# A transformer block with product-key experts: bf16 gate tables, a shorter candidate list, and another spread of gathered rows

## The chip, the cores and the metric

The kernel runs on one core of a Trainium2 chip. The metric is the device time of one launch in microseconds. TensorE multiplies matrices and writes PSUM, VectorE and ScalarE do elementwise work, GpSimd issues the indirect gathers and some other transfers, and SyncE issues most loads. Each engine works through its own instructions in order and waits on semaphores for the others.

## The reference

One layer on 528 frames (16 meta tokens ahead of 512 frames) of width 2048: two attention branches with gates, an output projection, and then the part that this change touches, a product-key expert layer (PEER), followed by a last RMSNorm. For each of the 512 tokens and each of 8 heads:

```
q  = (xb @ w_q)                        # 8 heads, two halves of 128
s  = q . sub_keys                      # per head two lists of 128 scores
s1, i1 = top_k(s[0], 16); s2, i2 = top_k(s[1], 16)
cand   = s1[:, None] + s2[None, :]     # 256 sums
top_s, pos = top_k(cand, 16)
idx = (i1[:, None] * 128 + i2[None, :])[pos]      # 16 of 16384 experts
g   = softmax(top_s)
h   = u[idx] . xb ;  act = g * gelu(h)
out = sum(act * v[idx])
```

So every token uses 8 x 16 = 128 experts of 16384, each with a row of `u` and a row of `v` of 2048 fp32 values (128 MB for each of the two tables). Both sorted lists fall, so the 16 highest sums (a, b) have (a + 1)(b + 1) <= 16.

## The kernel before

The kernel goes through the stages one after another: projections and stick-breaking attention, MLA attention, the branch products, the output projection, the routing scores, and two long expert phases. Every fp32 product is made of three fp32r matmuls on high and low halves (`mm3`, L230 to L232): ScalarE rounds a raw weight tile to the high half `wh` (L218), VectorE subtracts it for the low half `wl` (L219), and both are ready some tiles ahead of TensorE (four raw buffers, three of `wh` and `wl` and one more from an extra pool).

The expert layer is done in two ways. For `ND` = 342 of the 512 tokens (tiles 0, 1 and 2, the last one 86 tokens long) it is dense: all of `u` and all of `v` pass through TensorE, and the chosen experts come in as a gate matrix of 16384 experts by 342 tokens that is zero but for 128 entries a token. The other 170 tokens (128 of tile 3 and 42 spread over 126 partitions) gather their rows: `send` (L1135) fetches row k of each token by an indirect transfer on GpSimd's queue, and `row_step` multiplies it on VectorE, for `u` with a sum (L1148) and for `v` added into `xg` or `xgb` (L1152). There are 171 row steps for `u` and 171 for `v`.

The first phase (the loop over `e`, 128 turns) takes the tiles of `u`: two half tiles a turn, each 24 matmuls with 342 columns, a GELU on ScalarE and a store to `h_d`. Beside it run generators, of which the loop takes a step at fixed places:

- `routing` (`route`, for tiles 2, 0 and 1, two heads at a time). It forms the 256 sums `cand` (L889), takes the 16 highest in two rounds of eight with `top16` (five scans, L853 to L857), splits each place by shift and mask into its two indices, and finds the keys by one-hot comparison, product and sum (L901, L903, L905). Tile 3 is routed earlier, beside the scores, as `early`.
- `gating` (`gates_of`). For four tokens VectorE compares the two key lists with an iota (L1043, `[2, 4, 128]` in fp32), ScalarE scales the first one-hot by the high and low part of the weight (L1040), and TensorE multiplies, per token, the one-hot of the second keys as the stationary operand with the two scaled ones (L1051), which gives 128 x 128 gates in a bank of PSUM, with the tokens outermost. `gate_out` copies a bank to SBUF with the tokens innermost (L1073) and sends it to `g_d`.
- `rows_due`, which calls `row_step` so that the number of row steps follows the piecewise line `PACE` over the position in the loop: 10 by position 14, 175.5 by 124, `NU` = 181 at the end, so ten steps of `v` fall into this phase. Up to row `OWN` = 172 the buffers of the second phase serve as row buffers; behind it there are two.

The second phase (`STEPS`, 256 blocks of two columns) takes the tiles of `v`, multiplies them with the gated activations (`gated`, L1180 and L1182; `group_split`, L236) and adds into `acc` (L1321, L1323). Its row steps follow `(done - NU) * 484 / (342 - NU)` over the count n of columns, with a third row buffer from the pool `vp` for every third row. After step 490 TensorE folds `yvb` and `yv` in, and the final norm follows.

The order of instructions on each engine is made by a list scheduler from the order of recording and from the buffers; order that the text forces with `add_manual_dep` (rows behind a mark, gate work behind the GELU) is kept.

Of the kernel before, what the change touches and what calls it, by code (L numbers as in the profile page):

```python
# [57 lines left out]

CONST = {}


def _constants():
    p = np.arange(P)
    cols = {
        "ident": np.eye(P),
        "ones": np.ones((P, P)),
        "tri": (p[:, None] >= p[None, :]),
        "perm": (p[:, None] == (p[None, :] ^ 32)),
        "neg": np.where(p[None, :] <= p[:, None], NEG, 0.0),
        "qlo": np.where(p[None, :] < 64, 1.0, 0.0) * np.ones((P, 1)),  # L70
        "negrow": np.full((P, 64), NEG),
        "freq": (10000.0 ** (-((p % 32) / 32.0)))[:, None],
        "sign": np.where(p % 64 < 32, -1.0, 1.0)[:, None],
        "iota": np.arange(TOPK)[None, :] * np.ones((P, 1)),
        "sel": (p[:, None] // RB == np.arange(NB)[None, :]),
        "eps": np.full((P, 1), EPS),
        "halfpi": np.full((P, 1), math.pi / 2),
    }
    out, o = [], 0
    for k, v in cols.items():  # L80
        v = np.asarray(v, np.float64).astype(np.float32)
        CONST[k] = (o, o + v.shape[1])
        o += v.shape[1]
        out.append(v)
    return np.ascontiguousarray(np.concatenate(out, axis=1))

# [29 lines left out]
def _layout(x, positions, meta_tokens, norm_mix_g, w_in, mla_q_norm_g, mla_w_uq, mla_kv_norm_g,  # L116
# [50 lines left out]
    for i, n in enumerate(FRONT):  # L167
# [9 lines left out]
    return {"front": front, "ut": c(ut), "vb": c(vb), "u": c(u), "v": c(v), "xt": c(xt),  # L177
            "pos": c(pos[None]), "gains": c(gains), "const": CONST_ARR,
            "iota": c(np.broadcast_to(np.arange(P, dtype=np.float32), (P, P)))}
# [12 lines left out]
def body(tc, nc, a, dbg=None):  # L192
# [56 lines left out]
    SP.dma_start(gn, a["gains"])  # L249
    cst = cp.tile([P, CONST_ARR.shape[1]], F32, name="cst")  # L250

    def C(k):
        return cst[:, CONST[k][0]:CONST[k][1]]

# [29 lines left out]
    mixer = ExitStack()  # L284
    mp = mixer.enter_context(tc.tile_pool(name="mixer", bufs=1, side="left"))
    tri_r = mp.tile([P, P], F32R, name="tri_r")
    ones_r = mp.tile([P, P], F32R, name="ones_r")
# [31 lines left out]
    with tc.tile_pool(name="load", bufs=3, side="right") as lp:  # L319
# [31 lines left out]
    SP.dma_start(cst, a["const"])  # L351
    V.tensor_copy(tri_r, C("tri"))
# [434 lines left out]
    hgl = hgp.tile([P, KC, SEQ], F32R, name="hgl")  # L787
    rh_ = hgp.tile([P, SEQ], F32, name="rh_")
    rcol = hgp.tile([P, 1], F32, name="rcol")
    rcolb = hgp.tile([P, 1], F32, name="rcolb")  # L790

    with tc.tile_pool(name="outp", bufs=2, side="right") as op:
# [8 lines left out]
        for m in range(KC):  # L801
# [23 lines left out]
            gr = (op if m < KC - 1 else hgp).tile([P, 2, P], F32, name="gr")  # L825
            V.tensor_scalar(gr[:, 0], xr[:, TA:], gm, None, ALU.mult)
# [39 lines left out]
    def spread_rows():  # L866
# [10 lines left out]
        SP.dma_start(gwb[:PB], gwb_d.rearrange("t (r k) -> (t r) k", r=RB))  # L877

    def route(ti, n, pool):
        shp = [P, n, TOPK, TOPK]  # L880
        tv = pool.tile([P, H, TOPK], F32, name="tv", bufs=1)
        ef = keys[ti] = pool.tile([P, 2, H, TOPK], F32, name="ef", bufs=1)
        for h0 in range(0, H, n):
            hs = slice(2 * h0, 2 * (h0 + n))
            vv, ii = (t[:, ti, hs].rearrange("p (h c) k -> p h c k", c=2) for t in (v1, i1))
            i1f = pool.tile([P, n, 2, TOPK], F32, name="i1f", bufs=1)
            V.tensor_copy(i1f, ii)
            cand = pool.tile([P, n, TOPK, TOPK], F32, name="cand", bufs=1)
            V.tensor_tensor(cand, vv[:, :, 0, :, None].to_broadcast(shp), vv[:, :, 1, None, :].to_broadcast(shp), ALU.add)  # L889
            yield  # L890
            tp = pool.tile([P, n, TOPK], U32, name="tp", bufs=1)
# [3 lines left out]
            for c, (op_, arg) in enumerate(((ALU.logical_shift_right, 4), (ALU.bitwise_and, 15))):  # L895
                pu = pool.tile([P, n, TOPK], U32, name="pu", bufs=1)
                pf = pool.tile([P, n, TOPK], F32, name="pf", bufs=1)
                V.tensor_scalar(pu, tp, arg, None, op_)
                V.tensor_copy(pf, pu)
                oh = pool.tile([P, n, TOPK, TOPK], F32, name="oh", tag="cand", bufs=1)  # L900
                V.tensor_tensor(oh, pf[:, :, :, None].to_broadcast(shp), iota[:, None, None, :].to_broadcast(shp), ALU.is_equal)  # L901
                yield
                V.tensor_tensor(oh, oh, i1f[:, :, c, None, :].to_broadcast(shp), ALU.mult)  # L903
                yield
                V.reduce_sum(ef[:, c, h0:h0 + n], oh, axis=AX.X)  # L905
                yield
        e_ = pool.tile([P, H, TOPK], F32, name="e_", bufs=1)
# [15 lines left out]
    with tc.tile_pool(name="score", bufs=2, side="left") as sp_, \  # L923
# [9 lines left out]
        def scores(hc, qh, ql):  # L933
# [10 lines left out]
            if hc % 4 == 3:  # L944
                for _ in range(9):
                    next(early, None)
# [63 lines left out]

    iota_n = up.tile([P, P], F32, name="iota_n", bufs=1)
    SP.dma_start(iota_n, a["iota"])
    iota_b = iota_n[:, None, None, :].to_broadcast([P, 2, 4, P])
    gb = {}

    spare = [t[:, :, ND:ND + P].rearrange("p (i c t) k -> p i c t k", i=2, c=2) for t in (hgh, hgl)]

# [4 lines left out]
    def gates_of(ti):  # L1022
        ef, idx = keys[ti], up.tile([P, 2, P], F32, name="idx", bufs=1)
        wt = up.tile([P, 2, P], F32R, name="wt", bufs=1)
# [4 lines left out]
        S.activation(idx, ps[:, :2 * P].rearrange("p (c t) -> p c t", c=2), AF.Copy)  # L1029
        split(wt[:, 0], wt[:, 1], ps[:, 2 * P:3 * P])  # L1030
        yield
        n = min(P, ND - ti * P)
        for t0 in range(0, n + 4, 4):
            w, w_ = min(4, n - t0), min(4, n - t0 + 4)
            if t0:
                p0 = t0 - 4
                oh_, wo_ = (spare[c][:, p0 // 4 % 2] for c in range(2))
                for t in range(w_):
                    for c in range(2):
                        after_gelu(S.activation(wo_[:, c, t], oh_[:, 0, t].bitcast(F32), AF.Copy,  # L1040
                                                scale=wt[:, c, p0 + t:p0 + t + 1].bitcast(F32)))
            if w > 0:
                V.tensor_tensor(spare[0][:, t0 // 4 % 2, :, :w], idx[:, :, t0:t0 + w, None].to_broadcast([P, 2, w, P]),  # L1043
                                iota_b[:, :, :w], ALU.is_equal)
            yield
            gate_out()
            if t0:
                ps = ps_tile()
                for t in range(w_):
                    for c in range(2):  # L1050
                        T.matmul(ps[:, t * P:(t + 1) * P], oh_[:, 1, t], wo_[:, c, t], start=c == 0, stop=c == 1)  # L1051
                banks.append((ps, ti * P + p0, w_))
            yield
            if w_ < 4:
                break

# [3 lines left out]
    def gate_out(hold=3):  # L1060

        for _ in range(min(2, len(banks))):
# [9 lines left out]
            for hf, half in enumerate(gb["now"]):  # L1072
                after_gelu(S.activation(half[:, :, o:o + w].rearrange("p i t -> p t i"),  # L1073
                                        ps.rearrange("p (t f i) -> p f t i", t=4, f=2)[:, hf, :w], AF.Copy))
# [194 lines left out]
    for i, step in enumerate(STEPS):  # L1269
# [17 lines left out]
        for qi, (g, q8) in enumerate(step):  # L1287
# [18 lines left out]
            for dc in range(2):  # L1306
# [46 lines left out]
```

## Time and profile before

| | |
|---|---|
| median of three runs | 3632.78 us (3629.29 to 3633.52) |
| profiled execution | 3635.84 us, span 3634.1 us |
| mean granted TensorE clock | 0.994 |
| matmuls | 21139, busy 3573.3 us |
| VectorE, ScalarE, GpSimd busy | 2609.7, 1466.1, 743.5 us |
| moved | 890 MB, 245 GB/s over the span |
| first expert phase | about 1541 to 2626 us |
| second expert phase | about 2626 to 3600 us |

The profile is one execution. Its page groups instructions by source line, engine and operation and gives for each group the count, the busy time, the mean of one in ns, and the time in which the engine stood idle just before them with what ended that. A busy time by stretch gives the same for windows of the span, with the clock that TensorE was granted and the share of the DMA engines' time. Matmuls overlap in the pipeline, so the time that one occupies TensorE is read from the distance of two starts in the timeline and not from its length.

### The profile page before, as it was taken

The numbers are of one execution on the slowest core, as the hardware profiler recorded it, in microseconds if no ns is written. First come the engines' busy times: TensorE is split into PE (matmuls) and PEld (weight loads), VectorE is DVE, ScalarE is ACT, GpSimd is POOL, SyncE is SP. The second block draws the span as 40 slices with busy tenths as digits, with TensorE's granted clock in tenths as the row PEclk, the third lists the DMA queues.
The fourth block names the chain that finished last, engine by engine and source line by source line (L and its number), as shares of the span: only waits on it lengthen the run. The fifth ranks groups of instructions, "written<-read, shape, count | busy, mean of one in ns | idle before, by whom it ended". The sixth has DMA issues, their size and how long they took to land.

```text
span 3634.1 us, 53241 instructions
## 1 busy us (share of the span) xinstructions
PE 3573.3 (98%) x21139; PEld 3323.5 (91%) x21139; DVE 2609.7 (72%) x3431; ACT 1466.1 (40%) x2336; POOL 743.5 (20%) x523
## 2 busy tenths in 40 slices
PE   9999999999999999999999999999999999999998
PEld 8988888888788887899999999999999999999997
DVE  5533334345554558799999988887688988888886
ACT  4233323334443233234665666664323333333333
POOL 1000000000011122211232323333123333332320
PEclk9999999999999999999999999999999999999999
DMA  4222222221134443268899999999999999999983
GB/s 169 102 96 99 93 99 93 94 101 47 46 131 136 148 146 104 93 251 327 320 361 346 353 375 370 362 378 381 346 372 379 380 379 376 373 370 374 373 339 113
DMA packets 218385, 889.97 MB, mean 245 GB/s; under 512 B 24644, under 2 KB 47384, under 8 KB 174360
## 3 DMA queue, kind: packets, MB, share of 16 engines
q1 hardware_dynamic: 133016, 462.87, 35.0%
q0 software_dynamic: 56608, 384.51, 27.0%
q10 hardware_dynamic: 28512, 39.20, 3.0%
q8 instruction: 165, 2.70, 0.3%
q14 instruction: 84, 0.69, 0.1%
HBM read 824.18 MB, written 62.30 MB: 244 GB/s over the span
## 4 chain that ended last, share of the span: by engine, by line
PE 83%; DVE 9%; DMA 5%; issue 2%; ACT 1%; POOL 0%; SPq 0%; DVEq 0%; ACTq 0%; POOLq 0%
PE ps L230 26%; PE ps L231 26%; PE ps L232 26%; DVE row L1148 2%; DMA row<-v,eo 2%; DVE wl L219 2%; PE ps L1051 1%; DVE xg L1152 1%; DVE hgh L1043 1%; DMA hin<-h_d 1%; DMA wr<-vb 1%; DMA wr<-ut 0%; PE ps L707 0%; PE ps L716 0%; DMA hres<-ht_d 0%
## 5 line engine op out<-in xcount | busy, mean ns | idle before, releaser
L218 ACT ACTIVATE wh<-wr 128x1024 fp32r<-128x1024 f32 (+1 forms) x756 | 789.6, 1054 | 1505.9 <-PE ps L232 1313.5
L219 DVE TENSOR_TENSOR wl<-wr,wh 128x1024 fp32r<-128x1024 f32 (+1 forms) x741 | 935.7, 1268 | 440.7 <-ACT wh L218 438.6
L230 PE MATMUL ps<-hgh,wl 128*128 128x342 f32 (+1 forms) x2304 | 759.0, 329 | 17.8 <-DVE wl L219 15.4
L231 PE MATMUL ps<-hgl,wh 128*128 128x342 f32 (+1 forms) x2304 | 761.0, 330 | 0.9 <-DVE hgl L236 0.9
L232 PE MATMUL ps<-hgh,wh 128*128 128x342 f32 (+1 forms) x2304 | 755.0, 328 | 0.0
L230 PE MATMUL ps<-vah,wl 128*128 128x342 f32 x2048 | 657.9, 321 | 12.2 <-DVE wl L219 12.2
L231 PE MATMUL ps<-val,wh 128*128 128x342 f32 x2048 | 655.7, 320 | 0.0
L232 PE MATMUL ps<-vah,wh 128*128 128x342 f32 x2048 | 654.2, 320 | 0.0
L230 PE MATMUL ps<-xh,wl 128*128 128x512 f32 (+1 forms) x1376 | 470.3, 342 | 6.1 <-ACT xh L323 6.1
L231 PE MATMUL ps<-xl,wh 128*128 128x512 f32 (+1 forms) x1376 | 470.0, 342 | 0.2 <-DVE xl L324 0.2
L232 PE MATMUL ps<-xh,wh 128*128 128x512 f32 (+1 forms) x1376 | 468.0, 340 | 0.0
L230 PEld LDWEIGHTS ps<-hgh,wl 128*128 128x128 f32 x2304 | 435.3, 189 | 34.7 <-DVE wl L219 20.7
L232 PEld LDWEIGHTS ps<-hgh,wh 128*128 128x128 f32 x2304 | 436.2, 189 | 11.0 <-issue 0.2
L231 PEld LDWEIGHTS ps<-hgl,wh 128*128 128x128 f32 x2304 | 436.0, 189 | 11.1 <-DVE hgl L236 1.9
L230 PEld LDWEIGHTS ps<-vah,wl 128*128 128x128 f32 x2048 | 387.3, 189 | 14.2 <-DVE wl L219 14.2
L231 PEld LDWEIGHTS ps<-val,wh 128*128 128x128 f32 x2048 | 388.7, 190 | 0.0
L232 PEld LDWEIGHTS ps<-vah,wh 128*128 128x128 f32 x2048 | 387.4, 189 | 0.0
L1135 POOL DMA_INDIRECT row<-v,eo x128 | 220.8, 1725 | 543.1 <-DVE xg L1152 486.1
L1152 DVE SCALAR_TENSOR_TENSOR xg<-row,act,xg 128x2048 f32<-128x2048 f32 x127 | 298.0, 2346 | 36.2 <-DMA row<-v,eo 36.2
L1148 DVE SCALAR_TENSOR_TENSOR row<-row,xg 128x2048 f32<-128x2048 f32 x128 | 292.4, 2284 | 4.0 <-DMA row<-u,eo 4.0
L230 PEld LDWEIGHTS ps<-xh,wl 128*128 128x128 f32 x1376 | 259.5, 189 | 38.1 <-ACT xh L323 6.5
L1135 POOL DMA_INDIRECT row<-u,eo x128 | 179.2, 1400 | 537.7 <-DVE row L1148 474.2
(457 smaller groups left out, 4748.6 us busy)
## 6 DMA issues: line engine op xcount, KB each, us to landing
wr<-ut SPq DMA_DIRECT2D x256, 512.0 KB, 7.9
wr<-vb SPq DMA_DIRECT2D x256, 512.0 KB, 6.9
wr<-front SPq DMA_DIRECT2D x238, 512.0 KB, 3.2
g_d<-gb POOLq DMA_DIRECT2D x44, 512.0 KB, 12.0
gin<-g_d SPq DMA_DIRECT2D x32, 704.0 KB, 8.0
h_d<-hb ACTq DMA_DIRECT2D x128, 171.0 KB, 6.5
hin<-h_d SPq DMA_DIRECT2D x32, 684.0 KB, 8.3
gates<-gt ACTq DMA_DIRECT2D x32, 256.0 KB, 2.0
```

The source lines that it names most:

```text
L218: more["last"] = S.activation(hi[:, s], raw[:, s], AF.Copy)
L219: more["lo"] = (eng or V).tensor_sub(lo[:, s], raw[:, s], hi[:, s].bitcast(F32))
L230: T.matmul(ps, wl, xh, start=start, stop=False)
L231: T.matmul(ps, wh, xl, start=False, stop=False)
L232: T.matmul(ps, wh, xh, start=False, stop=stop)
L1043: V.tensor_tensor(spare[0][:, t0 // 4 % 2, :, :w], idx[:, :, t0:t0 + w, None].to_broadcast([P, 2, w, P]), iota_b[:, :, :w], ALU.is_equal)
L1051: T.matmul(ps[:, t * P:(t + 1) * P], oh_[:, 1, t], wo_[:, c, t], start=c == 0, stop=c == 1)
L1135: G.indirect_dma_start(out=row, out_offset=None, in_=a[src], in_offset=bass.IndirectOffsetOnAxis(ap=idx, axis=0))
L1148: ins = V.scalar_tensor_tensor(row, row, 1.0, x, ALU.mult, ALU.mult, accum_out=w)
L1152: ins = V.scalar_tensor_tensor(y, row, w, y, ALU.mult, ALU.add)
```

## The change

- `route` takes four heads at a time in the first expert phase (two in the early one). Of the 256 sums only 112 are formed: for the first four of the first list all 16 of the second, and for the other twelve the first four of the second. The scans run over 112 elements. The place is then taken apart with a table `first` (where each row of the 112 starts), comparison by `>=` and differences of the keys (`step`) for the first key, and with masks for the second. The scratch tiles keep one size, `[P, 512]`.
- `gates_of` works in bf16 and on two tokens at a time. Keys and iota lie as bf16 in `gr_last`, the iota with each number twice, so that the innermost dimension of the comparison is the pair of tokens. The weight is split into three bf16 parts; ScalarE makes the products with the first two (two a token, as before), VectorE makes that with the last (`last`). TensorE makes three matmuls a token instead of two, one step later than before. The stationary one-hot is read with a step of two elements, and the bank of PSUM has the four tokens innermost, as the copy in `gate_out` wants them. Three one-hot buffers are used: two in `rh_` and `more_oh`.
- The rows are spread otherwise. `NU` becomes 179 (two steps move to the second phase), `OWN` 170, `PACE` has a point more (75 steps at position 60), and in the second phase `PACE_V` asks for 19.5 steps by n = 64 and 163 by n = 488.
- The constants are split into two tiles, of which the one for the attention is freed with its pool (`cst_m`). The iota for the gates comes through a raw weight buffer.

```diff
     def route(ti, n, pool):
...
-            cand = pool.tile([P, n, TOPK, TOPK], F32, name="cand", bufs=1)
-            V.tensor_tensor(cand, vv[:, :, 0, :, None].to_broadcast(shp), vv[:, :, 1, None, :].to_broadcast(shp), ALU.add)
+            cand = pool.tile([P, 512], F32, name="cand", bufs=1)[:, :n * 112].rearrange("p (h x) -> p h x", x=112)
+            for x0, a0, na, nb in ((0, 0, 4, 16), (64, 4, 12, 4)):
+                V.tensor_tensor(cand[:, :, x0:x0 + na * nb].rearrange("p h (a b) -> p h a b", b=nb),
+                                vv[:, :, 0, a0:a0 + na, None].to_broadcast([P, n, na, nb]),
+                                vv[:, :, 1, None, :nb].to_broadcast([P, n, na, nb]), ALU.add)
+            step = pool.tile([P, 4, TOPK], F32, name="step", bufs=1)[:, :n]
+            V.tensor_copy(step[:, :, :1], i1f[:, :, 0, :1])
+            V.tensor_sub(step[:, :, 1:], i1f[:, :, 0, 1:], i1f[:, :, 0, :TOPK - 1])
...
-                top16(tv[:, h0 + h], tp[:, h], cand[:, h].rearrange("p a b -> p (a b)"), 256)
+                top16(tv[:, h0 + h], tp[:, h], cand[:, h], 112)
...
+            V.tensor_copy(pf, tp)
+            V.tensor_scalar(pu, tp, 15, None, ALU.bitwise_and)
+            V.tensor_copy(pb, pu)
+            V.tensor_scalar(pu, tp, 12, None, ALU.bitwise_and)
+            V.tensor_copy(p12, pu)
+            V.scalar_tensor_tensor(p12, pf, 64.0, p12, ALU.is_ge, ALU.mult)
+            V.tensor_sub(pb, pb, p12)
+            for c, (place, table, op_) in enumerate(((pf, C("first"), ALU.is_ge), (pb, iota, ALU.is_equal))):
+                for h in range(0, n, 2):
...
     def gates_of(ti):
...
+        S.activation(keys_b, ps[:, :2 * P].rearrange("p (c t) -> p c t", c=2), AF.Copy)
+        w, rest = ps[:, 2 * P:3 * P], ps[:, 3 * P:]
+        V.tensor_copy(last_b, w)
+        V.tensor_copy(wt[:, 0], last_b)
+        V.tensor_sub(rest, w, wt[:, 0])
+        V.tensor_copy(last_b, rest)
+        V.tensor_copy(wt[:, 1], last_b)
+        V.tensor_sub(last_b, rest, wt[:, 1])
...
+                        after_gelu(S.activation(wos[:, (p - 1) % 2, c, :, t], ohs[(p - 1) % 3][:, 0, :, t], AF.Copy,
+                                                scale=wt[:, c, t0 - 2 + t:t0 - 1 + t]))
+            if p < n // 2:
+                V.tensor_tensor(ohs[p % 3], keys_b[:, :, None, t0:t0 + 2].to_broadcast([P, 2, P, 2]),
+                                iota_b[:, None].to_broadcast([P, 2, P, 2]), ALU.is_equal)
+                V.tensor_tensor(last[:, p % 3], ohs[p % 3][:, 0], last_b[:, None, t0:t0 + 2].to_broadcast([P, P, 2]), ALU.mult)
...
+                    bank = ps_tile().rearrange("p (k t) -> p k t", t=4)
+                for t in range(2):
+                    o = (p - 2) % 2 * 2 + t
+                    for c, x in enumerate((last[:, (p - 2) % 3, :, t], wos[:, p % 2, 1, :, t], wos[:, p % 2, 0, :, t])):
+                        T.matmul(bank[:, :, o], ohs[(p - 2) % 3][:, 1, :, t], x, start=c == 0, stop=c == 2)
...
-                after_gelu(S.activation(half[:, :, o:o + w].rearrange("p i t -> p t i"),
-                                        ps.rearrange("p (t f i) -> p f t i", t=4, f=2)[:, hf, :w], AF.Copy))
+                after_gelu(S.activation(half[:, :, o:o + w], ps[:, hf * NK // 2:(hf + 1) * NK // 2, :w], AF.Copy))
...
-            yield from route(ti, 2, rk)
+            yield from route(ti, 4, rk)
...
-    NU = NR + 10
-    PACE = (2, 14, 124, NK - 0.5), (0, 10, 175.5, NU)
-    OWN = 172
+    NU = NR + 8
+    PACE = (2, 14, 60, 124, NK - 0.5), (0, 10, 75, 173.5, NU)
+    PACE_V = (0, 64, 488), (0, 19.5, 2 * NR - NU)
+    OWN = 170
...
-                while gs["done"] < len(todo) and n >= (gs["done"] - NU) * 484.0 / (len(todo) - NU):
+                while gs["done"] < len(todo) and gs["done"] - NU <= np.interp(n, *PACE_V):
```

More of the change, by code (lines that the diff above doesn't have):

```diff
@@ L74, in _constants @@
         "iota": np.arange(TOPK)[None, :] * np.ones((P, 1)),
+        "first": np.where(np.arange(TOPK) < 4, 16 * np.arange(TOPK), 48 + 4 * np.arange(TOPK))[None, :] * np.ones((P, 1)),
         "sel": (p[:, None] // RB == np.arange(NB)[None, :]),
@@ L78, in _constants @@
     }
[L79 to L85, printed above, removed]
+    out = []
+    for part in range(2):
+        arrs, o = [], 0
+        for k, v in cols.items():
+            if (k in MIXER_CONST) == bool(part):
+                v = np.asarray(v, np.float64).astype(np.float32)
+                CONST[k] = (part, o, o + v.shape[1])
+                o += v.shape[1]
+                arrs.append(v)
+        out.append(np.ascontiguousarray(np.concatenate(arrs, axis=1)))
+    return out
 CONST_ARR = _constants()
@@ L890, in route @@
             yield
-            tp = pool.tile([P, n, TOPK], U32, name="tp", bufs=1)
+            tp = pool.tile([P, 4, TOPK], U32, name="tp", bufs=1)[:, :n]
             for h in range(n):
-                top16(tv[:, h0 + h], tp[:, h], cand[:, h].rearrange("p a b -> p (a b)"), 256)
+                top16(tv[:, h0 + h], tp[:, h], cand[:, h], 112)
                 yield
[L895 to L906, printed above, removed]
+            pf, pb = (pool.tile([P, 4, TOPK], F32, name=x, bufs=1)[:, :n] for x in ("pf", "pb"))
@@ new lines, in route @@
+            V.tensor_sub(pb, pb, p12)
+            yield
+            for c, (place, table, op_) in enumerate(((pf, C("first"), ALU.is_ge), (pb, iota, ALU.is_equal))):
+                for h in range(0, n, 2):
+                    oh = pool.tile([P, 512], F32, name="oh", tag="cand", bufs=1).rearrange("p (h k a) -> p h k a", h=2, k=TOPK)
+                    key = step[:, h:h + 2] if c == 0 else i1f[:, h:h + 2, 1]
+                    V.tensor_tensor(oh, place[:, h:h + 2, :, None].to_broadcast(shp), table[:, None, None, :].to_broadcast(shp), op_)
+                    yield
+                    V.tensor_tensor(oh, oh, key[:, :, None, :].to_broadcast(shp), ALU.mult)
+                    yield
+                    V.reduce_sum(ef[:, c, h0 + h:h0 + h + 2], oh, axis=AX.X)
+                    yield
@@ L944, in scores @@
             if hc % 4 == 3:
-                for _ in range(9):
+                for _ in range(10):
                     next(early, None)
@@ L1007, in body @@
     up = stage.enter_context(tc.tile_pool(name="up", bufs=2, side="left"))
-    iota_n = up.tile([P, P], F32, name="iota_n", bufs=1)
-    SP.dma_start(iota_n, a["iota"])
-    iota_b = iota_n[:, None, None, :].to_broadcast([P, 2, 4, P])
     gb = {}
-    spare = [t[:, :, ND:ND + P].rearrange("p (i c t) k -> p i c t k", i=2, c=2) for t in (hgh, hgl)]
+    iota_f = raw_half()[:, :P]
+    SP.dma_start(iota_f, a["iota"])
+    iota_b = gr_last[:, 0].bitcast(BF16).rearrange("p (k t) -> p k t", t=2)
+    S.activation(iota_b, iota_f[:, :, None].to_broadcast([P, P, 2]), AF.Copy)
+    keys_b = gr_last[:, 1].bitcast(BF16).rearrange("p (c t) -> p c t", c=2)
+    more_oh = up.tile([P, 2, P, 2], BF16, name="more_oh", bufs=1)
+    ohs = list(rh_.bitcast(BF16).rearrange("p (i c k t) -> p i c k t", i=2, c=2, t=2)[:, i] for i in range(2)) + [more_oh]
+    wos = up.tile([P, 2, 2, P, 2], BF16, name="wos", bufs=1)
+    last = up.tile([P, 3, P, 2], BF16, name="last", bufs=1)
+    last_b = up.tile([P, P], BF16, name="last_b", bufs=1)
+    wt = up.tile([P, 2, P], F32, name="wt", bufs=1)
     def after_gelu(ins):
@@ L1022, in gates_of @@
     def gates_of(ti):
-        ef, idx = keys[ti], up.tile([P, 2, P], F32, name="idx", bufs=1)
-        wt = up.tile([P, 2, P], F32R, name="wt", bufs=1)
+        ef = keys[ti]
         ps = ps_tile()
@@ L1031, in gates_of @@
+        V.tensor_sub(last_b, rest, wt[:, 1])
         yield
         n = min(P, ND - ti * P)
[L1033 to L1038, printed above, removed]
-                    for c in range(2):
[L1040 to L1044, printed above, removed]
+        bank = None
@@ L1045, in gates_of @@
             yield
             gate_out()
[L1047 to L1055, printed above, removed]
+            if p > 1:
+                if p % 2 == 0:
+                    bank = ps_tile().rearrange("p (k t) -> p k t", t=4)
+                for t in range(2):
+                    o = (p - 2) % 2 * 2 + t
+                    for c, x in enumerate((last[:, (p - 2) % 3, :, t], wos[:, p % 2, 1, :, t], wos[:, p % 2, 0, :, t])):
+                        T.matmul(bank[:, :, o], ohs[(p - 2) % 3][:, 1, :, t], x, start=c == 0, stop=c == 2)
+                if p % 2 or p == n // 2 + 1:
+                    p0 = (p - 2) // 2 * 4
+                    banks.append((bank, ti * P + p0, min(4, n - p0)))
```

26 lines of the change are left out of this document (17 added, 9 removed).

## The prediction

> **What bounds the kernel now.** I read the page's head first, then busy time by stretch from the start of the expert loop, then who TensorE waited for.
>
> ```profile
> span 3634.1 us, 53241 instructions
> PE 3573.3 (98%) x21139; PEld 3323.5 (91%) x21139; DVE 2609.7 (72%) x3431; ACT 1466.1 (40%) x2336; POOL 743.5 (20%) x523
> ```
>
> TensorE has 61 us of idle time in all, so two things can move the end: the work on TensorE itself, and these gaps. The stretches, with the columns PE, PEld, DVE, ACT, POOL, granted clock, DMA share and GB/s:
>
> ```profile
> 1541.00:1707.00 166.00, 164.23 (x1011) 161.23 (x1010) 160.22 (x383) 58.27 (x70) 29.82 (x23) 0.99 0.73 273
> 1707.00:1850.00 143.00, 135.60 (x883) 132.46 (x882) 141.22 (x211) 92.72 (x202) 35.90 (x27) 1.00 0.89 323
> 1850.00:2000.00 150.00, 150.00 (x998) 149.94 (x997) 138.57 (x166) 93.88 (x208) 46.20 (x37) 1.00 0.96 365
> 2000.00:2040.00 40.00, 35.60 (x222) 34.48 (x221) 39.79 (x62) 27.42 (x57) 11.54 (x11) 0.97 0.93 351
> 2040.00:2490.00 450.00, 450.00 (x3005) 449.98 (x3005) 367.67 (x326) 302.70 (x681) 152.34 (x110) 1.00 0.96 367
> 2490.00:2600.00 110.00, 107.53 (x691) 107.25 (x690) 80.89 (x67) 37.60 (x47) 28.62 (x20) 1.00 0.96 382
> 2600.00:2850.00 250.00, 236.42 (x1456) 233.94 (x1456) 208.22 (x175) 74.41 (x71) 73.99 (x42) 0.97 0.95 365
> 2850.00:3550.00 700.00, 700.00 (x4456) 700.00 (x4455) 624.80 (x518) 225.52 (x209) 208.32 (x122) 1.00 0.95 369
> ```
>
> From 1541 to 1850 and from 2000 to 2040 VectorE is full (341 of 349 us) and TensorE has holes; from 2040 to 2490 and from 2850 on TensorE has none. Around the change of phase near 2600 VectorE isn't full and the holes come back. Who TensorE waited for, in 1700 to 2040 and then in 2585 to 2850 (total, times, longest):
>
> ```profile
> PE ps L230 <- DVE wl L219: 11.6, 15, 2.2
> PE ps L230 <- DVE wl L219: 16.0, 7, 5.2
> ```
>
> Both are the low half of a weight tile that VectorE delivers late: first because it has too much to do, then because it stands in its queue behind a gathered row that hasn't landed. These 28 us, a little refill after each, and the gate matmuls are all that the change can reach.
>
> **Gate matmuls.** Two fp32 matmuls a token become three bf16 ones. A 342-column matmul in an undisturbed stretch (one of three source lines; 1486 of 4458):
>
> ```profile
> 2850.00:3550.00 700.00, 473.00 (x1486) 279.90 (x1485) 1.00 0.95 369
> ```
>
> 700 / 4458 = 0.157 us from start to start, so 128 columns stream in 0.059. The gates before:
>
> ```profile
> 1723.47 1.01 PE L1051 MATMUL ps<-hgl,hgh 128*128 128x128 f32 x8
> 1724.31 0.37 PE L230 MATMUL ps<-hgh,wl 128*128 128x342 f32 x1
> 1724.52 0.33 PE L231 MATMUL ps<-hgl,wh 128*128 128x342 f32 x1
> ...
> L1051 PE MATMUL ps<-hgl,hgh x684: 222/275/281, 1723.5 to 2484.9; 128*128 128x128 f32 x171
> ```
>
> Eight take 0.84 us (0.105 each, not 0.059: the fp32 weight load sets the pace), and the next matmul takes 0.21 in place of 0.157. That is 0.893 for four tokens, 76.4 us for 85.5 fours. What bf16 costs between fp32 matmuls is in the attention:
>
> ```profile
> 271.21 0.29 PE L447 MATMUL ps<-qh,kl 128*128 128x272 f32 x1
> 271.34 0.23 PE L448 MATMUL ps<-bf 128*128 128x128 bf16 x1
> 271.38 0.37 PE L449 MATMUL ps<-ql,kh 128*128 128x272 f32 x1
> 271.59 0.28 PE L450 MATMUL ps<-qh,kh 128*128 128x272 f32 x1
> 271.71 0.23 PE L447 MATMUL ps<-qh,kl 128*128 128x144 f32 x1
> ...
> 272.08 0.22 PE L447 MATMUL ps<-qh,kl 128*128 128x16 f32 x1
> 272.16 0.18 PE L448 MATMUL ps<-bf 128*128 128x16 bf16 x1
> ...
> 272.42 0.48 PE L230 MATMUL ps<-xh,wl 128*128 128x512 f32 x1
> ...
> L448 PEld LDWEIGHTS <-bf x40: 94/95/98, 182.9 to 761.2; 128*128 128x128 bf16 x40
> ```
>
> Three fp32 matmuls of 272 columns (0.125 each) and one of bf16 take 0.50, so the bf16 one costs 0.125: the fp32 load behind it is no longer covered. In the 16-column group, three fp32 and one bf16 take 0.34, the three fp32 loads alone (3 x 0.11); there the bf16 load is hidden entirely. A burst of six (two tokens) is then 5 x 0.059 + 0.125 = 0.42 us, and 171 bursts are 71.7: **4.7 us less**. Ends: 0.04 each (L448's start to the next) gives 0.325 a burst, 20.8 less; the old fp32 pace of 0.11 gives 0.685, 40.7 more. I stay at 0.059, nearest to streaming. The stationary operand is now read with a step of two elements and the bank written with a step of four; no row shows either.
>
> **VectorE until 2040.**
>
> ```profile
> L1043 DVE TENSOR_TENSOR hgh<-idx,iota_n 128x1024 fp32r<-128x1024 f32 x85 | 103.5, 1219 | 1.6 <-PE ps L1051 1.2 <-ACT idx L1029 0.4
> L901 DVE TENSOR_TENSOR oh<-pf,cst 128x512 f32<-128x512 f32 x32 | 22.1, 690 | 0.7
> L236 DVE TENSOR_TENSOR knl<-ps,knh 128x264 fp32r<-128x264 f32 x16 | 6.3, 430 | 2.9 <-ACT knh L235 2.8
> L913 DVE TENSOR_TENSOR gw_all<-tv 128x128 f32<-128x128 f32 x4 | 1.1, 274 | 0.0
> L889 DVE TENSOR_TENSOR cand<-v 128x512 f32<-128x512 f32 x16 | 11.0, 685 | 0.0
> L856 DVE MAX8 tv<-wk 128x8 f32<-128x256 f32 x32 | 13.4, 420 | 0.3
> L856 DVE MAX8 v<-wk 128x8 f32<-128x128 f32 x64 | 18.1, 282 | 0.8
> L898 DVE TENSOR_SCALAR pu<-tp 128x32 uint32<-128x32 uint32 x32 | 6.1, 191 | 0.3
> L1148 DVE SCALAR_TENSOR_TENSOR row<-row,xg 128x2048 f32<-128x2048 f32 x128 | 292.4, 2284 | 4.0 <-DMA row<-u,eo 4.0
> ```
>
> Routing, a tile of 128 tokens: eight heads with five scans each fall from 256 to 112 elements, 0.42 to 0.265 (from 0.282 at 128), 40 x 0.15 = 6.0 us. The candidates fall from 4 x 0.685 to 2 x (0.43 + 0.36), 1.2 less. The small instructions at about 0.19 stay 20 (some are longer, 0.3 more), and the 24 one-hot instructions of 512 stay. 6.9 us a tile, 20.7 for the three tiles of this phase.
>
> Gates: one comparison of 1.22 for four tokens becomes two of 512 bf16 elements and two products of 256. At the fp32 time of as many elements this is 2 x (0.69 + 0.43) = 2.24; at that of as many bytes, 2 x (0.43 + 0.274) = 1.41. I take the bytes, as every operand is 16-bit and lies in adjacent pairs: 0.19 more; the upper end is 1.02 more. By the span of L1051 above, 316 of 761 us, 35.5 of the 85.5 fours lie before 2040: 6.7 more (or 36).
>
> No row before shows a two-source operation in bf16. [...]
>
> Rows: up to position 60 (about 2040) the pace falls from 10 + 46 x 165.5/110 = 79.2 to 75, 4.2 rows of 2.37 us with the accumulator read, 9.9 us.
>
> Sum by 2040: 20.7 - 6.7 + 9.9 = 24 us off VectorE, against 11.6 of waits and about 2.5 of refill. The load comes in bunches (score ranks and routing are already at 160 of 166 before the first gate), so I count **10 us less** at the end, 14 at most. At the upper price VectorE has 5 us more to do, and the waits would grow by that.
> After 2040 the same 0.19 (or 1.02) a four is 10 (or 51) us under 82 us of VectorE's idle time, so nothing; without that cover it would go onto the weight halves.
>
> **ScalarE.**
>
> ```profile
> L1073 ACT ACTIVATE gb<-ps 128x256 f32<-128x256 f32 x170 | 92.7, 668 | 0.0
> L1029 ACT ACTIVATE idx<-ps 128x256 f32<-128x256 f32 x3 | 1.2, 390 | 0.0
> ```
>
> The bank's copy writes four adjacent tokens now; between 390 and 668 ns, up to 47 us off ScalarE, which has 147 of 450 us free in the middle stretch: nothing on the path. Its 684 scalings stay in number.
>
> **Change of phase.** Two rows move from the first phase to the second; the last rows of the first phase keep 5.5 in 3.5 positions and two buffers. The third row buffer of the second phase lies in memory that the last store of the first phase reads:
>
> ```profile
> 2634.17 0.94 POOL L1135 DMA_INDIRECT row<-v,eo  x1 [11.41 <-DMA acc<-ht_d]
> 2642.47 2.35 DVE L1152 SCALAR_TENSOR_TENSOR xg<-row,act,xg 128x2048 f32<-128x2048 f32 x1 [5.50 <-DMA row<-v,eo]
> DVE xg L1152 <- DMA row<-v,eo: 21.6, 11, 5.5
> ```
>
> Before, this gather (row 183, as n % 3 == 0) is the third row of the phase; now row 180 is the second, wanted three half tiles (5.7 us) sooner. One weight half stands ahead of it in the new program's order, which gives back 24 x 0.157 = 3.8: some 3 us longer. The next rows come 6.2 us apart, not 5.7 (19.5 in place of 21.3 in 64 steps), which takes perhaps 2 off the other six waits. **1 us more**, between 10 less and 12 more.
>
> **The rest.** The constants in two transfers, the iota through a weight buffer, and routing's 40 steps in the score stage: under 10 us before use or in stages that end in no wait of theirs: nothing. The last row is due at step 486, not 481; TensorE needs it at 490, 4 x 12 x 0.157 = 7.5 us later, against 2.4 us of work: nothing, 2 us if two rows are queued there.
>
> **Sum.** -4.7 - 10 + 1 = -13.7 us. The profiled execution took 3635.84 (span 3634.1 and 1.7 around it), so 3622; the median of the runs, 3632.78, is 3.1 lower, so **3619 us**, 0.4% faster.
>
> **Rivals.**
> - The weight loads pace the bf16 burst: strided, one behind another, they don't hide, and a matmul costs L448's whole load, 0.095. Then 5 x 0.095 + 0.125 = 0.60, 171 bursts 102.6 us, 26 more than before and 31 above my term: **3650**. For it: the fp32 gates are paced so. Against: the 16-column group. From 0.075 it eats the whole gain, from 0.083 it is slower than before by over 0.2%. Hidden by half (0.077) it is 0.51 a burst, 87.2 us, 15.5 above my term: 3635. [...]
> - VectorE runs the bf16 pairs at the fp32 rate: waits grow by 5 in place of falling by 10: **3634**. For it: no row at a double rate with two sources. Against: half the bytes.
> - The second row of the new phase holds the queue for longer, with the half clock that the 0.97 around 2600 shows: 10 us more, **3629**.
> - All early waits and the refills go and the phase change gains 10: **3604**.
>
> **How the numbers follow.** Mine 0.45 (own range 3609 to 3628), the load rival 0.12 at 0.095 or worse and 0.11 half hidden, fp32 rate 0.10, phase change 0.10, all waits 0.12. 0.2% is 7.3 us, about what a measurement here can tell from none: faster ends at 3625.5, slower begins at 3640. Faster: 0.41 + 0.12 + 0.03 = 0.56; same: 0.04 + 0.09 + 0.05 + 0.06 = 0.24; slower: 0.02 + 0.12 + 0.05 + 0.01 = 0.20. The range of 3600 to 3645 leaves out the worst loads and a larger gain at both ends.
>
> **What would show it.** Six bf16 matmuls about 0.42 us from the burst's first to the next fp32 one; comparisons near 0.43 and products near 0.28; under 5 us of TensorE's waits in 1700 to 2040; one wait of about 8 near 2640. Wrong would be me if the burst takes over 0.5, the comparisons 0.69, or the waits around 2600 to 2850 change by over 8.

## The result, and the profile after

The changed kernel takes 3665.39 us (median of 4 runs, 3655.95 to 3667.88) against 3631.75 for the kernel before in the same comparison: a ratio of 1.0086, 95% interval 1.0073 to 1.0099. It is 0.9% slower, where 0.4% faster was forecast.

The head of its page, and then its busy time by the stretches shown of before (PE, PEld, DVE, ACT, POOL, granted clock, DMA share, GB/s):

```profile
span 3666.1 us, 54318 instructions
PE 3611.2 (99%) x21481; PEld 3348.6 (91%) x21481; DVE 2596.6 (71%) x3726; ACT 1437.9 (39%) x2334; POOL 711.1 (19%) x523
```

```profile
1541.00:1707.00 166.00, 164.23 (x1019) 162.22 (x1018) 155.39 (x392) 60.51 (x75) 30.56 (x23) 0.99 0.76 286
1707.00:1850.00 143.00, 143.00 (x960) 139.23 (x959) 136.14 (x261) 88.72 (x208) 33.73 (x27) 1.00 0.89 327
1850.00:2000.00 150.00, 150.00 (x1003) 146.37 (x1002) 128.57 (x210) 86.92 (x198) 39.99 (x35) 1.00 0.92 339
2000.00:2040.00 40.00, 40.00 (x271) 38.88 (x270) 33.47 (x47) 24.73 (x60) 11.68 (x11) 1.00 0.90 340
2040.00:2490.00 450.00, 450.00 (x3024) 437.80 (x3023) 355.83 (x463) 270.98 (x649) 122.02 (x103) 1.00 0.94 349
2490.00:2600.00 110.00, 107.17 (x677) 105.98 (x676) 78.07 (x73) 39.29 (x60) 26.87 (x22) 0.98 0.93 357
2600.00:2850.00 250.00, 233.15 (x1441) 230.51 (x1440) 197.28 (x165) 75.59 (x76) 73.07 (x39) 0.97 0.94 353
```

VectorE's load fell, as forecast, and TensorE has no idle time left from 1707 to 2490. The span grew all the same, and TensorE's busy time by 37.9 us: the loss is in TensorE's own work. In 1700 to 2040, where TensorE had waited 11.6 us for `wl`, the view lists no wait any more. From 2490 to 2850, where before had 16.0 us, stands this (total, times, longest):

```profile
PE ps L236 <- DVE wl L225: 19.6, 10, 7.4
```

The timeline of TensorE shows where the time went, at one burst of gates, the matmul ahead of it, the one behind it, and the start of the next burst:

```profile
2003.33 0.32 PE L238 MATMUL ps<-hgh,wh 128*128 128x342 f32 x1
2003.49 0.29 PE L1096 MATMUL ps<-last,rh__9426 128*128 128x128 bf16 x1
2003.58 0.42 PE L1096 MATMUL ps<-wos,rh__9426 128*128 128x128 bf16 x2
2003.80 0.31 PE L1096 MATMUL ps<-last,rh__9426 128*128 128x128 bf16 x1
2003.91 0.42 PE L1096 MATMUL ps<-wos,rh__9426 128*128 128x128 bf16 x2
2004.08 0.40 PE L236 MATMUL ps<-hgh,wl 128*128 128x342 f32 x1
...
2007.95 0.28 PE L1096 MATMUL ps<-last,more_oh 128*128 128x128 bf16 x1
```

From burst to burst are 4.46 us. Between them stand 24 matmuls of 342 columns, 24 x 0.1575 = 3.78, so six bf16 matmuls cost 0.68 us; the mean over all 171 bursts, counted in the same way, is 0.675. Forecast was 0.42. That is 115.4 us for all gates, not 71.7.

VectorE's pieces have the sizes of the forecast, and ScalarE's copy of the bank is a little shorter than forecast:

```profile
L1085 DVE TENSOR_TENSOR rh__9426<-gr_last 128x512 bf16<-128x512 bf16 x115 | 48.6, 422 | 44.6 <-PE ps L1096 44.3
L1087 DVE TENSOR_TENSOR last<-rh__9426,last_b 128x256 bf16<-128x256 bf16 x115 | 32.6, 286 | 1.2
L1117 ACT ACTIVATE gb<-ps 128x256 f32<-128x256 f32 x170 | 52.1, 366 | 0.0
L863 DVE FIND_INDEX8 tp<-tv,cand 128x8 uint32<-128x112 f32 x26 | 7.0, 269 | 0.0
```

### The profile page after: what moved, and what is told of

It is laid out like the page before. It is cut to its first block, busy times and chain, and to the rows that moved or that the text cites. A ratio compares the mean times of both kernels' runs of the same rounds, so it can differ in the third digit from the quotient of the medians.

```text
span 3666.1 us, 54318 instructions
## 1 busy us (share of the span) xinstructions
PE 3611.2 (99%) x21481; PEld 3348.6 (91%) x21481; DVE 2596.6 (71%) x3726; ACT 1437.9 (39%) x2334; POOL 711.1 (19%) x523
## 4 chain that ended last, share of the span: by engine, by line
PE 82%; DMA 6%; issue 5%; DVE 4%; POOL 1%; ACT 1%; SPq 0%; DVEq 0%; POOLq 0%; ACTq 0%
PE ps L236 26%; PE ps L238 25%; PE ps L237 25%; PE ps L1096 3%; DMA row<-v,eo 3%; DMA hin<-h_d 1%; DVE xg L1196 1%; DVE wl L225 1%; POOL row L1179 1%; DMA wr<-vb 1%; DMA row<-v,eob 0%; DVE xgb L1196 0%; DMA gin<-g_d 0%; PE ps L715 0%; DMA g_d<-gb 0%
## 5 line engine op out<-in xcount | busy, mean ns | idle before, releaser
L236 PE MATMUL ps<-hgh,wl 128*128 128x342 f32 (+1 forms) x2304 | 774.0, 336 | 11.1 <-DVE wl L225 8.8
L236 PEld LDWEIGHTS ps<-hgh,wl 128*128 128x128 f32 x2304 | 443.8, 193 | 23.4 <-DVE wl L225 10.5
L237 PEld LDWEIGHTS ps<-hgl,wh 128*128 128x128 f32 x2304 | 438.4, 190 | 11.4 <-DVE hgl L242 1.9
L237 PEld LDWEIGHTS ps<-xl,wh 128*128 128x128 f32 x1376 | 259.5, 189 | 31.9 <-DVE xl L331 1.3
```

The source lines that it names most:

```text
L236: T.matmul(ps, wl, xh, start=start, stop=False)
L237: T.matmul(ps, wh, xl, start=False, stop=False)
```

## The experiments

### Which access makes the bf16 matmuls slow

The stationary operand is read with a step of two elements, the moving one too, and the bank is written with a step of four. The first four kernels make each dense by itself, and then all.

```diff
 e1:  T.matmul(bank[:, :, o], ohs[..][:, 1].rearrange("p k t -> p (k t)")[:, t * P:(t + 1) * P], x, ...)
 e2:  x -> x.rearrange("p k t -> p (k t)")[:, t * P:(t + 1) * P]
 e3:  bank = ps_tile();  T.matmul(bank[:, o * P:(o + 1) * P], ohs[..][:, 1, :, t], x, ...)
      and the copy of the bank turned as in the kernel before
 e4:  all three
```

> The changed kernel with one edit: the stationary one-hot is read as 128 adjacent elements (64 keys of both tokens) and not with a step of two (128 keys of one token), so the gates are other numbers; count, shapes and everything else stay. In the changed kernel the six matmuls of a burst start 0.097 to 0.109 us apart. Theory A (a stationary operand read with a step of two loads slowly and is not hidden): start to start falls to about 0.06, 171 bursts x 6 x 0.045 = 46 us at most, some 3620 to 3630. Theory D (a bf16 load behind another matmul is not hidden, whatever its layout): nothing changes, 3660 to 3668. Theories B (moving operands) and C (the bank) also expect no change here.

> The changed kernel with one edit: the three moving operands (last, wos) are read as 128 adjacent elements (64 keys of both tokens) and not with a step of two, so the gates are other numbers. Theory B (the moving operand with a step of two streams at half rate): the six matmuls start about 0.06 us apart in place of 0.105, some 3620 to 3630. Theories A, C and D: no change, 3660 to 3668.

> The changed kernel with one edit that keeps the whole computation: the bank of PSUM has the four tokens outermost, so that a matmul writes 128 adjacent elements and not every fourth, and the copy of the bank turns the order as in the kernel before (668 ns in place of the shorter one, on ScalarE, off the path). Theory C (the write with a step of four slows the matmul): start to start about 0.06, some 3620 to 3630. Theories A, B and D: no change, 3660 to 3670.

> The three edits of the runs beside it together (stationary and moving operands and the bank all read and written as 128 adjacent elements; the gates are other numbers). If any layout is the cause, alone or with another, start to start falls to about 0.06 and the time to 3615 to 3630. Theory D (the bf16 loads themselves set the pace): it stays at about 0.1, and the time at 3655 to 3668.

One run each: 3665.75, 3661.28, 3617.70 and 3616.00 us, with 3637.43 for the kernel before. The first bf16 matmul of a burst and the first fp32 one behind it, of e1, of e2 and then of e4:

```profile
2003.99 0.29 PE L1096 MATMUL ps<-last,rh__9426 128*128 128x128 bf16 x1
...
2004.58 0.40 PE L236 MATMUL ps<-hgh,wl 128*128 128x342 f32 x1
```

```profile
2003.26 0.29 PE L1096 MATMUL ps<-last,rh__9426 128*128 128x128 bf16 x1
...
2003.84 0.40 PE L236 MATMUL ps<-hgh,wl 128*128 128x342 f32 x1
```

```profile
2003.38 0.23 PE L1096 MATMUL ps<-last,more_oh 128*128 128x128 bf16 x1
...
2003.70 0.40 PE L236 MATMUL ps<-hgh,wl 128*128 128x342 f32 x1
```

0.59 us with dense stationary operands, as in the changed kernel, 0.58 with dense moving ones, and 0.32 with everything dense. Only the bank counts: theory C. The steps of two in SBUF cost next to nothing: from start to start the six matmuls are 58.1 ns apart in e4 and 60.8 in e3, on the mean of all bursts.

Timed, the dense bank is faster than both kernels:

> The changed kernel with the tokens outermost in the bank, as in the run e3_bank_dense, now timed. If the strided write of the bank was the whole of the loss: 3615 to 3622, 0.3 to 0.5% faster than before, 48 less than the changed kernel.

3617.41 us, ratio 0.9956 (0.9942 to 0.9970). Its bursts:

```profile
2002.43 0.31 PE L238 MATMUL ps<-hgh,wh 128*128 128x342 f32 x1
2002.59 0.23 PE L1096 MATMUL ps<-last,rh__9426 128*128 128x128 bf16 x1
2002.66 0.28 PE L1096 MATMUL ps<-wos,rh__9426 128*128 128x128 bf16 x2
...
2002.91 0.40 PE L236 MATMUL ps<-hgh,wl 128*128 128x342 f32 x1
...
2006.79 0.23 PE L1096 MATMUL ps<-last,more_oh 128*128 128x128 bf16 x1
```

From burst to burst 4.20, less 3.78: 0.42 us (0.413 over all 171), the forecast's figure. The strided write costs 171 x (0.675 - 0.413) = 44.8 us, and the two medians lie 48.0 apart.

Two more ask what of the write is slow: a smaller step, and overwriting in place of adding.

```diff
 g4:  bank = ps_tile().rearrange("p (q k t) -> p q k t", q=2, t=2);  T.matmul(bank[:, o // 2, :, o % 2], ...)
 h3:  T.matmul(bank[:, :, o], ..., start=True, stop=True)
```

> The changed kernel with two tokens innermost in the bank and two halves of it outermost, so that a matmul writes every second element and not every fourth; the whole computation is kept. Theory P (the price grows with the step): start to start between 0.06 and 0.105, about 0.075, 3630 to 3640. Theory T (any step costs the same): 0.105, 3655 to 3666. Theory F (two adjacent elements of 4 bytes still go together): 0.06, 3615 to 3621.

> The changed kernel, in which each of a token's three matmuls overwrites its part of the bank in place of adding to it (so only the product with the first part of the weight is left, and the gates are rounded); the write keeps its step of four. Theory W (the write itself is slow with a step): start to start stays at 0.10 to 0.11, 3655 to 3668. Theory R (adding to what stands there is the slow part, as it reads and writes): about 0.06, 3612 to 3622.

3662.76 and 3668.51 us (one run each). The timelines of g4 and h3:

```profile
2000.80 0.29 PE L1096 MATMUL ps<-last,rh__9426 128*128 128x128 bf16 x1
...
2001.39 0.40 PE L236 MATMUL ps<-hgh,wl 128*128 128x342 f32 x1
```

```profile
2001.13 0.29 PE L1096 MATMUL ps<-last,rh__9426 128*128 128x128 bf16 x1
...
2001.72 0.40 PE L236 MATMUL ps<-hgh,wl 128*128 128x342 f32 x1
```

0.59 again in both: a step of two costs as much as one of four (theory T), and it is the write itself, not the adding (theory W).

### The parts one by one

```diff
 f2:  changed kernel, gates_of and the copy of the bank as before
 f3:  dense bank, NU, PACE, OWN and the rule of the second phase as before
 f4:  dense bank, route as before (256 sums, two heads at a time)
 g2:  dense bf16 gates alone (route and the spread of rows as before)
 g3:  route alone (gates and the spread of rows as before)
```

> The new routing and the new spread of rows with the gates of the kernel before (fp32, four tokens at a time, eight matmuls). Theory A (with a dense bank the bf16 gates are worth no more on TensorE than the fp32 ones, and the gain is VectorE's): 0.893 us for four tokens in place of 0.82, which is 6 more than the dense bank, less 8 if the 342-column matmuls go at 155.7 ns beside the fp32 bursts as they did before and not at 157.4: 3613 to 3621. Theory B (the bf16 gates themselves free VectorE or ScalarE, and the early waits hang on that): waits of 3 us or more come back before 2040, 3622 to 3630. It also tells whether 155.7 belongs to the fp32 bursts.

> The dense bank with the spread of rows of the kernel before (181 rows in the first phase, 79 by position 60, even steps in the second phase). VectorE then has 9.9 us more to do before 2040. Theory A (the shorter routing alone takes the early waits away): no wait before 2040 beyond 2 us, and the waits of 2490 to 2850 fall from 23 us to the 17 of before: 3611 to 3617. Theory B (the spread of rows is needed for it): 4 to 8 us of waits before 2040, 3617 to 3625.

> The dense bank with the routing of the kernel before (256 sums, two heads at a time). VectorE then has 20.7 us more to do in the three tiles before 2040. Theory A (the early waits hang on the routing): 8 to 12 us of them come back, 3626 to 3632. Theory B (the spread of rows does it): under 4 us of waits, 3616 to 3621. If the 6 us by which the first phase begins sooner come from the shorter list in the stage of the scores, they go too.

> The bf16 gates with the dense bank on the kernel before, with its routing and its spread of rows. By my sum VectorE has 6.7 us more to do before 2040 and the waits there (11.6 us) grow. Theory S (the sum of VectorE's work counts): 12 to 18 us of waits in 1700 to 2040, 3630 to 3638. Theory L (the length of one piece counts: a comparison of 1.22 us ahead of a weight half is replaced by pieces of 0.42 and 0.28, half as many of them at each step): under 3 us of waits, 3616 to 3624.

> The new routing on the kernel before, with its gates and its spread of rows. Theory S: 20.7 us less of VectorE's work before 2040, so under 4 us of waits there, 3620 to 3627. Theory L: the comparisons of 1.22 us stand where they stood, and 8 us of waits or more stay, 3627 to 3636.

| kernel | us | ratio to before | interval | waits 1700 to 2040, us |
|---|---|---|---|---|
| f1: dense gates, routing, rows | 3617.41 | 0.9956 | 0.9942 to 0.9970 | none |
| f3: dense gates, routing | 3616.94 | 0.9948 | 0.9933 to 0.9964 | none |
| f4: dense gates, rows | 3620.38 | 0.9956 | 0.9941 to 0.9972 | none |
| g2: dense gates | 3615.88 | 0.9951 | 0.9934 to 0.9967 | none |
| f2: routing, rows | 3628.84 | 0.9987 | 0.9977 to 0.9996 | 1.2 |
| g3: routing | 3626.62 | 0.9976 | 0.9967 to 0.9986 | 1.7 |

The waits of f2 and then of g3 in that stretch:

```profile
PE ps L236 <- DVE wl L225: 1.2, 2, 0.6
```

```profile
PE ps L236 <- DVE wl L225: 1.7, 3, 1.1
```

The dense gates alone give the whole gain, the routing alone half of it, and the spread of rows none that shows. f3 and f4 leave out one of these two each beside the dense gates, and lose nothing that shows. f2's time lies in the range of its theory B, but without that theory's waits (3 us or more; it has 1.2). Of the 11.4 us between f2 and f1, the fp32 gates are 6 on TensorE (0.895 us for four tokens in f2, 2 x 0.413 in f1, 85.5 times); the rest was not taken apart. By the sum of VectorE's work (theory S) g3 should have had under 4 us of waits, and has 1.7; but g2 should have had longer waits than before, and it has none. Theory L, that it is the length of one piece, fits g2 and not g3, where it had 8 us or more. It was tried by itself: the comparison of before was cut in two:

```diff
 h4:  V.tensor_tensor(spare[0][:, .., s:s + 2], ..)   # two tokens at each of the two steps of a four
```

> The kernel before with the comparison of the gates in two instructions of two tokens, one at each of the two steps of a four, in place of one of four tokens; the work is the same, 0.07 us more for a four at most. Theory L (the early waits hang on the length of one piece, 1.22 us, ahead of a weight half): under 4 us of waits in 1700 to 2040 in place of 11.6, 3620 to 3628. Theory S (they hang on the sum of the work): 10 to 15 us of waits, 3631 to 3638. Theory G (neither; something else in the bf16 gates took them away in g2): also 10 to 15 us.

3633.17 us, ratio 0.9999 (0.9989 to 1.0008), and in 1700 to 2040 as much waiting as before:

```profile
PE ps L230 <- DVE wl L219: 11.6, 13, 1.9
```

Theory L falls too. What the traces show instead is how much VectorE has in its queue for each half tile of weights. Groups of VectorE's instructions from 1707 to 1850, the `wl` row of before and of g2, and VectorE's busy time in that stretch in g2:

```profile
L219 DVE TENSOR_TENSOR wl<-wr,wh 128x1024 fp32r<-128x1024 f32 x31 | 37.5, 1217 | 0.8 <-ACT wh L218 0.8
```

```profile
L225 DVE TENSOR_TENSOR wl<-wr,wh 128x1024 fp32r<-128x1024 f32 x35 | 42.7, 1220 | 0.0
```

```profile
1707.00:1850.00 143.00, 142.53 (x244) 1.00 0.95 351
```

Before: 141.22 us for 31 halves, 4.56 each (h4: 142.11 for 31, 4.58). g2: 142.53 for 35, 4.07. g3: 141.86 for 34, 4.17. TensorE needs 24 x 0.1575 and one dense burst, 4.19; in before it is as much, 24 x 0.1557 and half a burst of eight (0.893 / 2), 4.18. So VectorE sets the pace of before and h4 and not that of g2, although it is as full there. It does less for each half there because routing is spread wider. Busy time of the one-hot tile `oh` of the routing, in 1707 to 1850 and 1850 to 2000, before and then g2:

```profile
1707.00:1850.00 143.00, 16.50 (x24) 1.00 0.89 323
1850.00:2000.00 150.00, 9.64 (x14) 1.00 0.96 365
```

```profile
1707.00:1850.00 143.00, 13.72 (x20) 1.00 0.95 351
1850.00:2000.00 150.00, 9.67 (x14) 1.00 0.99 379
```

24 pieces for 31 halves became 20 for 35. VectorE keeps to its written order (in before it stood idle for 5.50 us, up to 2642.47, for a gathered row, though TensorE waited from 2641.2 for a `wl` that stood behind that row and had its `wh` at 2632.16), so that ratio is the order's and not the waits'. Why the scheduler lays the routing thinner beside the bf16 gates is not settled, and no run forced that order alone: that the load for each half tile makes the waits is read from these traces, not shown by an experiment.

### A second pace of the 342-column matmuls

Beside the gates of before, a 342-column matmul took 155.7 ns (mean over the three source lines); in the changed kernels 157.4 to 157.8. f2 has the old fp32 bursts and not that pace (157.7, the mean of 66 from 2000 to 2012), so it isn't theirs. A second profile of the kernel before, and two kernels in which the tile of the constants is 64 bytes longer, so that every weight tile moves by 64 bytes:

```diff
 g1:  the kernel before, unchanged
 h2:  kernel before, cst = cp.tile([P, CONST_ARR.shape[1] + 16], ...)
 h1:  g2 (dense gates alone), the same 16 columns added
```

> The kernel before once more, for a second profile of it. Theory K (two things in its first profile are the kernel's own: 342-column matmuls at 155.7 ns on the mean of the three lines beside the gates, and a first expert phase that begins at 1562.7, where eight changed kernels began at 1554.7 to 1558.5): both come again. Theory E (they are draws of one execution): 157.4 to 157.8 ns, or a start below 1559. Waits for the low weight half in 1700 to 2040 come again with 9 to 14 us under both.

> The kernel before with the tile of the constants 64 bytes longer and nothing else changed. Theory A: 157.4 ns or more for a 342-column matmul beside the gates, 8 to 10 us longer than before, 3640 to 3648. Theory N: 155.7 ns, 3628 to 3639.

> The dense bf16 gates alone (as in g2) with the tile of the constants 64 bytes longer, so that the weight tiles behind it begin 64 bytes higher and stand to 128 bytes as in the kernel before. Theory A (the place of the weight tiles sets the pace of the 342-column matmuls, 155.7 ns in the kernel before and 157.4 to 157.8 in every changed one): 155.7 ns from about 1715 on, and 9 us less than g2, 3605 to 3609. Theory N (something else): 157.4 ns, 3612 to 3620.

g1 took 3632.73 us with 9.3 us of early waits, and had the pace of 155.7 again. The matmuls in 100 us without gates or waits, before and h2 in 2490 to 2590, then g2 and h1 in 1600 to 1700:

```profile
2490.00:2590.00 100.00, 100.00 (x645) 1.00 0.96 384
```

```profile
2490.00:2590.00 100.00, 100.00 (x636) 1.00 0.96 380
```

```profile
1600.00:1700.00 100.00, 100.00 (x637) 1.00 0.89 332
```

```profile
1600.00:1700.00 100.00, 100.00 (x645) 1.00 0.89 335
```

64 bytes take the faster pace from before (645 to 636) and give it to the bf16 gates (637 to 645): theory A for the pace. But the place alone doesn't set it. In 1600 to 1700, ahead of the first gates, the kernel before runs at the slower pace as well (636, in g1 and h2 too), and h4, whose edit moves no tile, at the faster one (645; and 1032 matmuls in 1541 to 1707, where before has 1011). What else counts beside the place stays open. For the time it holds in h1: 3608.98 us, ratio 0.9927 (0.9910 to 0.9943), about 7 below g2. In h2 it does not: 3634.95 in one run, since the first expert phase, 7 us longer, also begins 7.6 sooner (before, then h2):

```profile
1562.73 0.50 PE L230 MATMUL ps<-hgh,wl 128*128 128x342 f32 x1
```

```profile
1555.08 0.59 PE L230 MATMUL ps<-hgh,wl 128*128 128x342 f32 x1
```

Whether that start hangs on the 64 bytes too stays open: the kernel before itself began at 1562.7 and, in g1, at 1559.8, kernels with the place of before began at 1557.8 to 1562.7, the others at 1554.7 to 1559.1, and the two ranges overlap.

Last, both edits on the whole change:

> The changed kernel whole, with the dense bank and the 64 bytes behind the constants. If the two edits add: the dense bank (3617 in f1) less the 7 that the 64 bytes gave to the bf16 gates alone (h1 against g2), 3608 to 3613. If the faster pace of the 342-column matmuls hangs on the order of the kernel before beside the place of its tiles: 3614 to 3620.

3609.25 us, ratio 0.9930 (0.9914 to 0.9947): they add, and the pace in 1600 to 1700 goes from 636 in f1 to 645. h1 and i1 beat both kernels.

## Why the prediction was wrong, step by step

- **Gate matmuls: the step that failed.** "A burst of six (two tokens) is then 5 x 0.059 + 0.125 = 0.42 us, and 171 bursts are 71.7: 4.7 us less." Measured 0.675 and 115.4 us, 43.7 above the term, of a miss of 46. The mechanism was right and the dense bank runs at 0.413. What failed is that the step of four in the bank was noted, with no row to show it, and then priced at nothing; it costs 0.26 us a burst. The upper end of 0.685 (its own terms, 5 x 0.11 + 0.125, make 0.675) held the measured cost, but it was put down to the old fp32 pace and not to the write, and left to the 0.12 of the load rival. That rival came nearest in time (3650) and is wrong in cause: in e1 dense stationary operands change nothing (0.59 us from a burst's first matmul to the next fp32 one, as in the changed kernel). The matmuls of a burst are 0.104 us apart from start to start with the strided write and 0.061 with the dense one, on the mean of all bursts: that the write itself is slow should have been a rival. The dense 0.061 also lies below both prices of the load rival, 0.095 and 0.077.
- **VectorE until 2040: right in size, the cause incomplete.** 10 us of waits were to go, 11.6 went (the kernel before had 9.3 in g1). The prices were right: 0.42 and 0.29 for comparison and product, where the author's estimate from fp32 rows of as many bytes was 0.43 and 0.274, and 0.27 for a scan. The shorter routing alone takes the waits down to 1.7 us (g3), as the sum has it. But the waits don't follow the sum of VectorE's work over the stage: g2 takes none off, and they go.
- **ScalarE: right.** The copy fell from 668 to 366 ns, a little below the range, and nothing followed from it: in f1, with the dense bank, it is back at 672 ns, and the kernel is faster all the same.
- **Change of phase: in the range, but not clear of the spread.** 1 us more, between 10 less and 12 more; the waits from 2490 to 2850 grew by 3.6, and the one of "about 8 near 2640" is 7.4 us (it ends at 2683.6, as the second phase begins 31 us later than in the kernel before). But these sums differ as much from one execution to the next where the rows are those of before: 17.6 in g1, 19.4 in h4.
- **The rest, costed at nothing: two effects, of 11 and 6.5 us, that partly cancel.** With the smaller tile of constants the weight tiles lie elsewhere, and the pace of 155.7 ns is gone: about 5200 matmuls x 2.1 ns = 11 us more (i1 against f1 shows that 64 bytes bring it back). The first expert phase began 6.5 us sooner (1556.2); between two executions of the kernel before this start differs by 3 us, and its cause stays open.
- **The sum.** The burst's 43.7 above its term, 11 for the pace, less 6.5 for the start, less some 4 of early waits and refill beyond the 10, and some 3 around the change of phase make 47 above the forecast of 3622 for the profiled execution, which took 3667.88, 46 above.

## What to carry to other kernels

Write a matmul's output densely to PSUM where you can (here 0.061 us from start to start, 0.104 with a step), and let the copy out of the bank turn the order, on an engine with time to spare (here ScalarE, 672 ns a copy in f1 and 366 in the changed kernel). Price every access whose step changes, on the PSUM side first, even where no row shows it (here 0.26 us a burst there, and 3 ns a matmul at most for the steps in SBUF). Count an engine's load for each unit of the loop in its written order, not as a sum over a stage: a wait can go without any work being removed, as the 11.6 us did in g2. When a tile changes size, look at the pace of matmuls that the diff doesn't touch (here 155.6 or 157.8 ns, by 64 bytes).

## What the runs showed of the hardware

- A write to PSUM with a step of four fp32 elements took a 128-column bf16 matmul from 0.061 (f1) to 0.104 us from start to start (changed kernel), and a step of two costs as much (g4: 0.59 us from a burst's first matmul to the next fp32 one, as in the changed kernel, against 0.32 in f1); a step of two in both SBUF operands costs 3 ns at most (60.8 with it in e3, 58.1 without in e4).
- With a dense output, bf16 weight loads of 128 columns did not set the pace of matmuls of the same size: such a load lasts 95 ns in the kernel before (L448), and in f1 the matmuls of a burst start 61 ns apart (median 58).
- Moving the weight tiles by 64 bytes in SBUF changed the pace of 342-column fp32 matmuls by 1.4% (157.8 and 155.6 ns from start to start; 636 and 645 of them in 100 us), in three pairs: before and h2, g2 and h1, f1 and i1. The place alone doesn't set it, as the kernel before ran at both paces.
